# Thirty-one reciprocal roots of the feature norms, computed on GpSimd behind one VectorE step

## The chip, the cores and the metric

The program runs on one core of one Trainium2 chip. The metric is the device time of one execution in microseconds. Five engines work side by side, each through its own queue in order: TensorE (PE; its weight loads are listed as PEld), VectorE (DVE), ScalarE (ACT), GpSimd (POOL) and SyncE (SP), which issues most of the transfers.

## The reference, cut to what matters

Two transformer-like blocks follow each other on 512 tokens of 1024 features in float32, each block two layers deep. The second block also carries a context of 256 tokens. What matters here is the norm over the features that stands in front of and behind nearly every part:

```python
def rms_norm(x, g):
    x32 = x.astype(jnp.float32)
    y = x32 * lax.rsqrt(jnp.mean(x32 * x32, axis=-1, keepdims=True) + EPS)
    return (y * g.astype(jnp.float32)).astype(x.dtype)

for l in range(DEPTH):                       # first block
    h = rms_norm(x, g_norm1[l]) * (1.0 + sc1) + sh1
    ...                                      # two kinds of attention on h
    x = x + gt1 * (merged @ w_out[l])
    h = rms_norm(x, g_norm2[l]) * (1.0 + sc2) + sh2
    ...
    x = x + gt2 * ((jax.nn.silu(a) * v_ff) @ w_down[l])

for i in range(DEPTH):                       # second block
    hx = rmsnorm(x, norm_g[i, 0]) * (1.0 + sc_x) + sh_x
    ...                                      # convolution (i = 0, with a layer norm) or attention (i = 1)
    x = x + g_x * rmsnorm(yx, norm_g[i, 1])
    fx = rmsnorm(x, norm_g[i, 2]) * (1.0 + scf_x) + shf_x
    x = x + gf_x * rmsnorm(swiglu(fx, ffn_w1[i], ffn_w3[i], ffn_w2[i]), norm_g[i, 3])
```

The same is done to the context in the second block, as long as it is needed.

## The kernel before, in words

Activations are kept with the features on the partitions: x is eight tiles of 128 features by 512 tokens. Each matrix product is done three times on rounded halves (high by high, low by high, high by low). So every activation that enters a product is split into hh and hl (`modulate`, lines 268 to 275), and every weight chunk that arrives by DMA is split by `weights`: the high half by ScalarE on L166, the low half by VectorE on L167, up to 128x1024 elements at a time. Products are summed in PSUM by `dense` (L184, L187, L188) and `dense_tok` (L194 to L196).

Most norms are done for 256 tokens at a time, the first half (A) and the second (B) one after the other, or for the context's 256 tokens. A norm has these steps. ScalarE squares each of the eight feature tiles (L226), and VectorE adds the squares of the middle six to the first (L228). `rstd_psum` lets TensorE sum the two remaining tiles over the partitions against a column of 1/1024 (L244), which gives the mean squares as a 128x2 block in PSUM, one column for each 128 tokens. `rsqrt` takes their reciprocal roots with nine VectorE steps (L208 to L217): a scaled copy w, a first guess by arithmetic on the bits as integers, and two steps of iteration, each result written to small tiles rs_w, rs_y, rs_b and rs_c. TensorE then transposes each column, spread over 128 columns, back into a 128x256 block rb in PSUM (L248). `rstd` copies this to SBUF by ScalarE (L255), since GpSimd's share of the products is made from there. `times_rb` multiplies the feature tiles by it: five of eight by VectorE (L266), and the tiles 1, 3 and 5 by ScalarE with the scale (L263) and GpSimd (L264). After a `post_norm` the product is added to x (L828, again tiles 1, 3, 5 on GpSimd) and squared for the norm that comes next; after a `pre_norm` it is shifted, rounded (L274) and its rest taken (L275).

`rstd_psum` is called 31 times: once in front of everything, for 512 tokens at once (four columns, from `emit`), and 30 times for 256. `rsqrt` is called 11 times more, on sums over heads and latents (lines 419, 475, 501, 1156 and 1199), with 8 to 32 columns; those calls stay on VectorE.

The order of the instructions on each engine is not that of the program text. The text gives what depends on what; a planner (`schedule_with_timeline_sim=True`, L1642) lays the instructions out by its own estimates of their times, each on the engine that the text names, and each engine then runs its list in order, waiting on semaphores. So other matmuls may stand between L244 and L248, and other VectorE steps between the nine of a root. Where two tiles have the same tag, `bufs` says how many buffers take turns.

GpSimd's other work is the products L264 and additions L828, sums of gates (L711), parts of the rotary embeddings, and in the convolution the filter tiles (L1009) and the issue of some DMAs (L1014).

Of the kernel before, what the change touches and what calls it, by code (L numbers as in the profile page):

```python
# [12 lines left out]
F32 = mybir.dt.float32  # L13
F32R = mybir.dt.float32r
I32 = mybir.dt.int32
AF = mybir.ActivationFunctionType
ALU = mybir.AluOpType
# [3 lines left out]
P = 128  # L21
# [4 lines left out]
EPS = 1e-6  # L26
# [66 lines left out]
class Core:  # L93
# [105 lines left out]

    def rsqrt(self, v, n, scale=1.0, factor=1.0, step=False):  # L200
        nc = self.nc
        w = self.sm.tile([P, 32], F32, tag="rs_w", name="rs_w", bufs=2)
        y = self.sm.tile([P, 32], F32, tag="rs_y", name="rs_y", bufs=3)
        b = self.sm.tile([P, 32], F32, tag="rs_b", name="rs_b", bufs=2)
        c = self.sm.tile([P, 32], F32, tag="rs_c", name="rs_c", bufs=2)
        w, y, b, c = w[:, :n], y[:, :n], b[:, :n], c[:, :n]
        k = -0.5 / (3.375 * factor) ** 2
        nc.vector.tensor_scalar(w, v, scale * k, EPS * k, op0=ALU.mult, op1=ALU.add)  # L208
        nc.vector.tensor_scalar(y.bitcast(I32), w.bitcast(I32), -0.5, float(0x5F375A86 - 2**22 - 2**30),
                                op0=ALU.mult, op1=ALU.add)  # L210
        nc.vector.tensor_tensor(b, y, y, op=ALU.mult)
        nc.vector.tensor_tensor(b, b, w, op=ALU.mult)
        nc.vector.scalar_tensor_tensor(c, b, 5.0 / 3.0, b, op0=ALU.add, op1=ALU.mult)
        nc.vector.scalar_tensor_tensor(c, c, 1.25, y, op0=ALU.add, op1=ALU.mult)
        nc.vector.tensor_tensor(b, c, c, op=ALU.mult)
        nc.vector.tensor_tensor(b, b, w, op=ALU.mult)
        last = nc.vector.scalar_tensor_tensor(y, b, 2.0 / 3.0, c, op0=ALU.add, op1=ALU.mult)  # L217
        return (y, last) if step else y


    def square_sum(self, pool, sums, x, k):
# [10 lines left out]
    def rstd_psum(self, sums):  # L232

        nc = self.nc
        n = sums[0].shape[-1]
        nt = n // P
        if n <= 256:
            pb = self.at_psum("rb")
            ps = pb[:, 256:]
        else:  # L240
            ps, pb = self.mm_psum("ms"), self.mm_psum("rb")
        for t in range(nt):
            for i, sq in enumerate(sums):
                nc.tensor.matmul(ps[:, t : t + 1], lhsT=sq[:, t * P : (t + 1) * P], rhs=self.mean_col,  # L244
                                 start=(i == 0), stop=(i == len(sums) - 1))
        r, last = self.rsqrt(ps[:, :nt], nt, step=True)
        for t in range(nt):
            nc.tensor.transpose(pb[:, t * P : (t + 1) * P], r[:, t : t + 1].to_broadcast([P, P]), self.ident)  # L248
        return pb[:, :n], last

    def rstd(self, pool, sums):

        pb, _ = self.rstd_psum(sums)
        rb = pool.tile("rb")[:, : pb.shape[-1]]
        self.nc.scalar.copy(rb, pb)  # L255
        return pb, rb
# [1043 lines left out]
def emit(tc, a, out, stop=None):  # L1300
    nc = tc.nc
    with ExitStack() as ctx:
        core = Core(ctx, tc, a)
        dense_psum = ctx.enter_context(ExitStack())
        core.ps = dense_psum.enter_context(core.psum_pool("ps"))
        x, h, c = core.x, core.h, core.const
# [21 lines left out]
        with tc.tile_pool(name="rope", reuse_waits="tile", bufs=1) as rp:  # L1328
# [19 lines left out]
            with tc.tile_pool(name="start", reuse_waits="tile", bufs=1) as pp:  # L1348
                acc = pp.tile([P, S], F32, name="acc")
                for k in range(KD):  # L1350
                    nc.sync.dma_start(out=x[k], in_=a["xT"][k])
                    sq = acc if k == 0 else pp.tile([P, S], F32, tag="sq", name="sq", bufs=3)
                    nc.scalar.activation(sq, x[k], AF.Square)
                    if 0 < k < KD - 1:
                        nc.vector.tensor_tensor(acc, acc, sq, op=ALU.add)
                act = pp.tile([P, KD], F32, name="act")
                nc.scalar.activation(act, core.colrange("c"), AF.Silu)
                wide = pp.tile([P, KD, 32], F32, name="wide")
                nc.vector.tensor_copy(wide, act.unsqueeze(2).to_broadcast([P, KD, 32]))
                each = pp.tile([P, 1], F32, name="each")  # L1360
                nc.vector.tensor_reduce(each, core.ident.rearrange("p (a b) -> p a b", b=32)[:, :, 0], op=ALU.add, axis=AX.X)
                core.idle_products(20)
                rb, _ = core.rstd_psum([acc, sq])
                ups = {t: core.at_psum("lat") for t in range(TOK)}

                def blocks(p):


                    mds = []
                    for which in range(2):  # L1370
                        raw = pp.tile([P, KD, 256], F32, tag="raw", name="rawt", bufs=4)
                        nc.sync.dma_start(out=raw, in_=a["w_ada0"][p, which])
                        md = core.mm_psum("md")
                        for j in range(2):
                            for g in range(4):
                                k = 2 * g + j
                                nc.tensor.matmul(md[32 * g : 32 * g + 32, :256], lhsT=wide[:, k, :], rhs=raw[:, k, :],
                                                 start=(j == 0), stop=(j == 1))
                        rows = pp.tile([P, 256], F32, tag="rows", name="rows0", bufs=2)
                        nc.scalar.copy(rows, md[:, :256])  # L1380
                        mds.append((md, rows))
                    for which, (md, rows) in enumerate(mds):
                        for j in range(2):
                            nc.tensor.matmul(md[:, 256 + j : 257 + j], lhsT=rows[:, j * P : (j + 1) * P], rhs=each,
                                             start=True, stop=True)
                        f = 8 * (1 - which) + 2 * p
                        nc.vector.tensor_tensor(mod[:, f : f + 2], md[:, 256:258], bias0[:, f : f + 2], op=ALU.add)

                for p in range(4):
                    blocks(p)  # L1390
                    ks = slice(2 * p, 2 * p + 2)
                    nc.vector.scalar_tensor_tensor(g1[0][:, ks], mod[:, 8 + 2 * p : 10 + 2 * p], 1.0, core.colrange("g10")[:, ks],
                                                   op0=ALU.add, op1=ALU.mult)
                    wh, wl = core.chunk(a["w_lat"][0, p])
                    for kk in range(2):
                        k = 2 * p + kk
                        xs = pp.tile([P, S], F32, tag="xn", name="xn", bufs=2)
                        nc.vector.scalar_tensor_tensor(xs, x[k], g1[0][:, k : k + 1], rb, op0=ALU.mult, op1=ALU.mult)
                        nc.scalar.activation(h[k][0], xs, AF.Identity, bias=mod[:, k : k + 1])
                        nc.vector.scalar_tensor_tensor(h[k][1], xs, mod[:, k : k + 1], h[k][0], op0=ALU.add, op1=ALU.subtract)  # L1400
                        for t in range(TOK):
                            core.dense_tok(ups[t][:, :448], h[k], slice(t * P, (t + 1) * P),
                                           (wh[:, kk, :], wl[:, kk, :]), k == 0, k == KD - 1)
                crow = core.silu_row(rp, a["c"], "crow")
                core.side = chain(core.modulation_rows(a["w_adat"][0], [crow], bias0, [mod], [48], 16),
                                  core.modulation_rows(a["w_adat"][1], [crow], core.colrange("b_ada1"), [mods[1]], [16]))
                rope_tables(core, pp, cos, sin)
# [229 lines left out]
def build(arrays, stop=None):  # L1637
    nc = bacc.Bacc("TRN2", target_bir_lowering=False, num_devices=1)
    a = {k: nc.dram_tensor(f"in_{k}", v.shape, mybir.dt.from_np(v.dtype), kind="ExternalInput").ap()
         for k, v in arrays.items()}  # L1640
    out = nc.dram_tensor("out_x", (KD, P, S), F32, kind="ExternalOutput").ap()
    with tile.TileContext(nc, schedule_with_timeline_sim=True) as tc:  # L1642
        emit(tc, a, out, stop)
    return nc
# [8 lines left out]
```

## Time and profile before

| | |
|---|---|
| median of three runs | 3121.16 us (3118.2 to 3124.4) |
| the profiled execution | 3128.48 us |
| its span, first to last instruction | 3126.8 us |
| mean granted clock of TensorE in it | 0.977 of full |
| TensorE busy | 3005.0 us |
| VectorE busy | 2153.8 us |
| ScalarE busy | 1386.6 us |
| GpSimd busy | 252.6 us |

The profile is of a single execution. All times within it are microseconds from the span's start. A number in square brackets in a row of the timeline is idle time of that engine just before the instruction, and behind the arrow stands what ended it. TensorE's instructions overlap in the pipeline, so its rows can be longer than their distance. `x2` at the end of a row means that two like instructions are merged in it.

### The profile page before, as it was taken

To read this page: it belongs to the slowest core of one execution; us is meant where nothing else is said; L and a number is where in the kernel's file an instruction comes from. 1 tells how busy PE (TensorE), PEld (TensorE's weight loads), DVE (VectorE), ACT (ScalarE), POOL (GpSimd) and SP (SyncE) were. 2 spreads that over 40 slices of the span, in tenths; PEclk is the share of its full clock that TensorE was granted. 3 is DMA by queue.
4 is the path that set the end of the run, shared out by engine and by line. 5 is a ranking of instruction groups with operands and counts; after the bars stand their busy time and mean duration, and the time that the engine had idled before them with its cause. 6 is when DMAs were issued, how large, how long until landed. Compare 5 with 4: busy or idle time off the path is not lost.

```text
span 3126.8 us, 44991 instructions
## 1 busy us (share of the span) xinstructions
PE 3005.0 (96%) x17004; PEld 2550.3 (82%) x17004; DVE 2153.8 (69%) x4013; ACT 1386.6 (44%) x2532; POOL 252.6 (8%) x336
## 2 busy tenths in 40 slices
PE   8999999999899999999999899999998989999998
PEld 6776888888777698888886699888887767898887
DVE  5774778887676488999789683645578976672336
ACT  3534563335533556343562473222235556653223
POOL 0000200000100020000023120000001510110001
PEclk8999999999999999999999999999999989999999
DMA  6563356454466253333344343433473400243333
GB/s 240 174 218 108 122 169 213 153 180 121 153 208 196 74 173 123 121 107 109 101 150 122 122 151 106 124 98 125 148 238 118 135 28 21 81 149 108 94 101 122
DMA packets 128845, 422.42 MB, mean 135 GB/s; under 512 B 15602, under 2 KB 21362, under 8 KB 127603
## 3 DMA queue, kind: packets, MB, share of 16 engines
q1 hardware_dynamic: 125426, 414.00, 41.1%
q0 software_dynamic: 1280, 2.77, 0.3%
q10 hardware_dynamic: 1920, 2.77, 0.3%
q8 instruction: 134, 2.20, 0.3%
q14 instruction: 85, 0.69, 0.1%
HBM read 411.85 MB, written 2.10 MB: 132 GB/s over the span
## 4 chain that ended last, share of the span: by engine, by line
PE 79%; DVE 11%; ACT 4%; issue 2%; DMA 2%; POOL 1%; ACTq 0%; SPq 0%; DVEq 0%; POOLq 0%
PE dn L184 5%; PE dn L188 5%; PE dn L187 5%; PE up L184 5%; PE up L187 5%; PE up L188 5%; PE pa L184 4%; PE pa L187 4%; PE pa L188 4%; PE pv L188 3%; PE pv L184 3%; PE pv L187 3%; DVE wlo L167 3%; PE g L184 2%; PE g L187 2%
## 5 line engine op out<-in xcount | busy, mean ns | idle before, releaser
L166 ACT CAST whi<-raw 128x1024 fp32r<-128x1024 f32 (+4 forms) x622 | 599.1, 967 | 1017.1 <-PE dn L187 275.2
L167 DVE TENSOR_TENSOR wlo<-raw,whi 128x1024 fp32r<-128x1024 f32 (+4 forms) x622 | 706.3, 1138 | 376.6 <-ACT whi L166 365.0
L184 PE MATMUL dn<-hi,whi 128*128 128x256 f32 (+1 forms) x1088 | 360.5, 334 | 3.9 <-ACT whi L166 1.6
L188 PE MATMUL dn<-hi,wlo 128*128 128x256 f32 (+1 forms) x1088 | 358.4, 332 | 1.2 <-DVE wlo L167 1.0
L187 PE MATMUL dn<-lo,whi 128*128 128x256 f32 (+1 forms) x1088 | 359.2, 331 | 0.2 <-DVE lo L290 0.2
L184 PE MATMUL up<-hh,whi 128*128 128x512 f32 (+1 forms) x800 | 294.3, 369 | 5.9 <-ACT hh L274 3.5
L187 PE MATMUL up<-hl,whi 128*128 128x512 f32 (+1 forms) x800 | 294.0, 368 | 1.1 <-DVE hl L275 1.1
L188 PE MATMUL up<-hh,wlo 128*128 128x512 f32 (+1 forms) x800 | 293.5, 368 | 0.0
L184 PEld LDWEIGHTS dn<-hi,whi 128*128 128x128 f32 x1088 | 205.8, 190 | 26.1 <-ACT whi L166 6.5
L188 PEld LDWEIGHTS dn<-hi,wlo 128*128 128x128 f32 x1088 | 205.9, 190 | 22.6 <-DVE wlo L167 2.0
L187 PEld LDWEIGHTS dn<-lo,whi 128*128 128x128 f32 x1088 | 206.4, 190 | 19.9 <-DVE lo L290 0.4
L313 DVE SCALAR_TENSOR_TENSOR mjunk<-mraw,crow 128x1024 fp32r<-128x1024 f32 (+1 forms) x152 | 185.9, 1223 | 46.8 <-PE g L187 18.9
L264 POOL TENSOR_TENSOR hp<-hp,rb 128x256 f32<-128x256 f32 x90 | 74.5, 840 | 1764.8 <-ACT hp L263 1295.9
L184 PE MATMUL pa<-hh,whi 128*128 128x512 f32 (+1 forms) x496 | 179.4, 362 | 3.4 <-ACT hh L274 3.3
L184 PEld LDWEIGHTS up<-hh,whi 128*128 128x128 f32 x800 | 154.0, 193 | 30.4 <-ACT hh L274 4.1
L187 PE MATMUL pa<-hl,whi 128*128 128x512 f32 (+1 forms) x496 | 178.5, 360 | 0.3
L188 PE MATMUL pa<-hh,wlo 128*128 128x512 f32 (+1 forms) x496 | 177.5, 358 | 0.0
L187 PEld LDWEIGHTS up<-hl,whi 128*128 128x128 f32 x800 | 153.8, 192 | 25.4 <-DVE hl L275 1.8
L188 PEld LDWEIGHTS up<-hh,wlo 128*128 128x128 f32 x800 | 153.7, 193 | 23.9
L188 PE MATMUL pv<-hh,wlo 128*128 128x512 f32 (+1 forms) x432 | 152.0, 352 | 1.1 <-DVE wlo L167 1.1
L184 PE MATMUL pv<-hh,whi 128*128 128x512 f32 (+1 forms) x432 | 151.8, 351 | 0.0
L187 PE MATMUL pv<-hl,whi 128*128 128x512 f32 (+1 forms) x432 | 151.6, 351 | 0.0
(477 smaller groups left out, 6985.3 us busy)
## 6 DMA issues: line engine op xcount, KB each, us to landing
raw<-in_w SPq DMA_DIRECT2D x148, 512.0 KB, 3.5
mraw<-in_w_modt SPq DMA_DIRECT2D x112, 512.0 KB, 4.2
raw<-in_w_up SPq DMA_DIRECT2D x100, 512.0 KB, 3.4
mraw<-in_w_adat SPq DMA_DIRECT2D x80, 512.0 KB, 4.2
raw<-in_w_pw SPq DMA_DIRECT2D x56, 512.0 KB, 3.4
raw<-in_w_down SPq DMA_DIRECT2D x48, 448.0 KB, 3.4
raw<-in_w_g SPq DMA_DIRECT2D x32, 512.0 KB, 4.3
raw<-in_w_out SPq DMA_DIRECT2D x32, 512.0 KB, 3.4
```

The source lines that it names most:

```text
L166: nc.scalar.copy(hi[:, :n], raw[:, :n])
L167: nc.vector.tensor_tensor(lo[:, :n], raw[:, :n], hi[:, :n], op=ALU.subtract)
L184: first = mm(out, lhsT=hi[:, k, :], rhs=xh[:, cols], start=(k == 0), stop=False)
L187: mm(out, lhsT=hi[:, k, :], rhs=xl[:, cols], start=False, stop=False)
L188: self.last = mm(out, lhsT=lo[:, k, :], rhs=xh[:, cols], start=False, stop=(k == n - 1))
L264: nc.gpsimd.tensor_tensor(p, p, rb[1], op=ALU.mult)
L313: behind(nc.vector.scalar_tensor_tensor(junk, raw, 1.0, v, op0=ALU.mult, op1=ALU.mult, accum_out=d[:, f : f + 1]))
```

## The change

`rstd_psum` no longer calls `rsqrt` but a new function, `rsqrt_aside`. It does the scaled copy w on VectorE, since it is read from PSUM, and everything else on GpSimd. The arithmetic is the same, but each of VectorE's three fused steps (add, then multiply) becomes an addition of a constant and a multiplication, so there are eleven GpSimd steps in place of eight on VectorE. Its tiles are four columns wide and have tags of their own, two or three buffers each. The tiles of `rsqrt`, 32 columns wide, get one buffer less each, rs_c apart. Nothing reads the last instruction of the root that `rstd_psum` gave back, and it is gone.

```diff
     def rsqrt(self, v, n, scale=1.0, factor=1.0, step=False):
         nc = self.nc
-        w = self.sm.tile([P, 32], F32, tag="rs_w", name="rs_w", bufs=2)
-        y = self.sm.tile([P, 32], F32, tag="rs_y", name="rs_y", bufs=3)
-        b = self.sm.tile([P, 32], F32, tag="rs_b", name="rs_b", bufs=2)
+        w = self.sm.tile([P, 32], F32, tag="rs_w", name="rs_w", bufs=1)
+        y = self.sm.tile([P, 32], F32, tag="rs_y", name="rs_y", bufs=2)
+        b = self.sm.tile([P, 32], F32, tag="rs_b", name="rs_b", bufs=1)
...
+    def rsqrt_aside(self, v, n):
+        w = self.sm.tile([P, 4], F32, tag="ra_w", name="ra_w", bufs=2)[:, :n]
+        y = self.sm.tile([P, 4], F32, tag="ra_y", name="ra_y", bufs=3)[:, :n]
+        b = self.sm.tile([P, 4], F32, tag="ra_b", name="ra_b", bufs=2)[:, :n]
+        c = self.sm.tile([P, 4], F32, tag="ra_c", name="ra_c", bufs=2)[:, :n]
+        g = self.nc.gpsimd
+        k = -0.5 / 3.375 ** 2
+        self.nc.vector.tensor_scalar(w, v, k, EPS * k, op0=ALU.mult, op1=ALU.add)
+        g.tensor_scalar(y.bitcast(I32), w.bitcast(I32), -0.5, float(0x5F375A86 - 2**22 - 2**30), op0=ALU.mult, op1=ALU.add)
+        g.tensor_tensor(b, y, y, op=ALU.mult)
+        g.tensor_tensor(b, b, w, op=ALU.mult)
+        g.tensor_scalar(c, b, 5.0 / 3.0, None, op0=ALU.add)
+        g.tensor_tensor(c, c, b, op=ALU.mult)
+        g.tensor_scalar(c, c, 1.25, None, op0=ALU.add)
+        g.tensor_tensor(c, c, y, op=ALU.mult)
+        g.tensor_tensor(b, c, c, op=ALU.mult)
+        g.tensor_tensor(b, b, w, op=ALU.mult)
+        g.tensor_scalar(b, b, 2.0 / 3.0, None, op0=ALU.add)
+        g.tensor_tensor(y, b, c, op=ALU.mult)
+        return y
...
-        r, last = self.rsqrt(ps[:, :nt], nt, step=True)
+        r = self.rsqrt_aside(ps[:, :nt], nt)
         for t in range(nt):
             nc.tensor.transpose(pb[:, t * P : (t + 1) * P], r[:, t : t + 1].to_broadcast([P, P]), self.ident)
-        return pb[:, :n], last
+        return pb[:, :n]
```

The two callers of `rstd_psum` (in `rstd` and in `emit`) take one value in place of two.

## Rows read from the trace of the kernel before

**Rows 1.** The page's first part: busy us (share of the span) xinstructions.

```profile
PE 3005.0 (96%) x17004; PEld 2550.3 (82%) x17004; DVE 2153.8 (69%) x4013; ACT 1386.6 (44%) x2532; POOL 252.6 (8%) x336
```

**Rows 2.** Waits of TensorE: who <- for whom: us in total, times, longest us.

```profile
PE rb L244 <- DVE acc L228: 17.9, 5, 5.9
PE rb L248 <- DVE rs_y L217: 7.1, 3, 3.4
```

**Rows 3.** The tile rs_w: durations min/median/max in ns, first and last start.

```profile
L208 DVE TENSOR_SCALAR rs_w<-rb x30: 147/156/160, 387.9 to 3114.5; 128x2 f32<-128x2 f32 x30
```

**Rows 4.** Timelines of two calls: start us, us, engine, line, op, out<-in, shapes.

```profile
391.46 0.15 DVE L217 SCALAR_TENSOR_TENSOR rs_y<-rs_b,rs_c 128x2 f32<-128x2 f32 x1
394.15 0.38 PE L248 MATMUL rb<-ident,rs_y 128*128 128x128 f32 x2
...
3097.16 0.16 DVE L217 SCALAR_TENSOR_TENSOR rs_y<-rs_b,rs_c 128x2 f32<-128x2 f32 x1
...
3099.85 0.38 PE L248 MATMUL rb<-ident,rs_y 128*128 128x128 f32 x2
```

**Rows 5.** Chain of waits that ended last, in pieces: start us, us, what.

```profile
14.93 0.17 DVE rs_w L208
...
1846.48 0.62 DVE rs_c L214
...
3116.03 0.17 DVE rs_y L217
```

**Rows 6.** Timeline of VectorE, the last call's first and last step.

```profile
3114.46 0.16 DVE L208 TENSOR_SCALAR rs_w<-rb 128x2 f32<-128x2 f32 x1 [1.43 <-PE rb L244]
...
3116.03 0.16 DVE L217 SCALAR_TENSOR_TENSOR rs_y<-rs_b,rs_c 128x2 f32<-128x2 f32 x1
```

**Rows 7.** Timeline of GpSimd: steps with two tensors, one behind the other.

```profile
789.04 0.46 POOL L371 TENSOR_TENSOR tabq<-cos,rows 128x128 f32<-128x128 f32 x1 [9.82 <-DMA rows<-in_rows]
789.46 0.46 POOL L371 TENSOR_TENSOR tabq<-sin,rows 128x128 f32<-128x128 f32 x1
...
798.98 1.42 POOL L264 TENSOR_TENSOR hp<-hp,rb 128x256 f32<-128x256 f32 x2 [4.87 <-ACT hp L263]
```

**Rows 8.** Timeline of GpSimd in the first microsecond: fills, then a select.

```profile
0.35 0.10 POOL L1638 MEMSET const-float32-1.0<- 128x1 f32 x1
...
0.81 0.20 POOL masks.py:197 MEMSET ident<- 128x128 f32 x1 [0.29 <-POOLq L1638]
1.09 0.29 POOL masks.py:199 TENSOR_SCALAR_AFFINE_SELECT ident<-ident 128x128 f32<-128x128 f32 x1
```

**Rows 9.** Timelines of GpSimd and VectorE where each is slowed.

```profile
427.79 2.71 POOL L264 TENSOR_TENSOR hp<-hp,rb 128x256 f32<-128x256 f32 x2 [26.62 <-ACT hp L263]
427.81 1.22 DVE L167 TENSOR_TENSOR wlo<-raw,whi 128x1024 fp32r<-128x1024 f32 x1
...
2498.03 1.30 POOL L1185 TENSOR_TENSOR stk<-qf,stk 128x512 f32<-128x512 f32 x1
2498.13 1.22 DVE L212 TENSOR_TENSOR rs_b<-rs_b,rs_w 128x8 f32<-128x8 f32 x1
```

**Rows 10.** Timeline of TensorE: transposes that waited for a root.

```profile
16.73 1.11 PE L248 MATMUL rb<-ident,rs_y 128*128 128x128 f32 x4 [1.84 <-DVE rs_y L217]
...
797.40 0.69 PE L248 MATMUL rb<-ident,rs_y 128*128 128x128 f32 x2 [3.42 <-DVE rs_y L217]
```

**Rows 11.** Timeline of VectorE behind the call at 1597.3.

```profile
1598.99 1.23 DVE L167 TENSOR_TENSOR wlo<-raw,whi 128x1024 fp32r<-128x1024 f32 x1
...
1600.47 1.22 DVE L167 TENSOR_TENSOR wlo<-raw,whi 128x1024 fp32r<-128x1024 f32 x1
```

**Rows 12.** Three stretches: busy us (x) of each engine, granted clock, DMA.

```profile
1840.00:1850.00 10.00, 5.85 (x25) 5.16 (x25) 8.74 (x32) 5.74 (x16) 2.33 (x3) 0.59 0.29 102
2412.00:2419.00 7.00, 4.12 (x16) 3.37 (x16) 5.47 (x24) 3.51 (x9) 1.42 (x2) 0.50 0.06 24
2737.00:2747.00 10.00, 8.13 (x38) 7.44 (x38) 8.72 (x33) 6.27 (x15) 3.44 (x5) 0.54 0.19 54
```

More of the change, by code (lines that the diff above doesn't have):

```diff
@@ L245, in rstd_psum @@
                                  start=(i == 0), stop=(i == len(sums) - 1))
-        r, last = self.rsqrt(ps[:, :nt], nt, step=True)
+        r = self.rsqrt_aside(ps[:, :nt], nt)
         for t in range(nt):
             nc.tensor.transpose(pb[:, t * P : (t + 1) * P], r[:, t : t + 1].to_broadcast([P, P]), self.ident)
-        return pb[:, :n], last
+        return pb[:, :n]
     def rstd(self, pool, sums):
-        pb, _ = self.rstd_psum(sums)
+        pb = self.rstd_psum(sums)
         rb = pool.tile("rb")[:, : pb.shape[-1]]
@@ L1362, in emit @@
                 core.idle_products(20)
-                rb, _ = core.rstd_psum([acc, sq])
+                rb = core.rstd_psum([acc, sq])
                 ups = {t: core.at_psum("lat") for t in range(TOK)}
```

## The prediction

> **What bounds the kernel now.** I read the page first: TensorE is busy 96% of the span, VectorE 69%, GpSimd 8% [rows 1]. So a step costs time only where TensorE waits for it. TensorE's waits come next [rows 2]: for a finished reciprocal root (L248) it waited 7.1 us in three places, for the sums in front of one (L244) 17.9 us in five. The change touches 31 calls, 30 of two columns [rows 3] and the first one of four. In the timelines I set the end of L217 against the start of the transposes L248 in each call. In 21 of the 31 the transposes came 1.2 us or more behind the root, with other matmuls between; the first is at 391.6 to 394.15, the last at 3097.3 to 3099.85 [rows 4]. In the other ten the root is nearly or wholly waited for. Along the chain of waits I added up the pieces named after the roots' tiles: 52 pieces, from 14.93 to 3116.03, make 8.2 us for these 31 calls [rows 5], of which 1.6 us lie in the first call, 1.6 us in the last, 1.0 us near 795, and nearly all the rest where two norms follow each other. That, not VectorE's total, is what can be won.
>
> **What goes from VectorE.** The last call runs alone: nine steps, 3114.46 to 3116.19, one every 0.196 us, 0.16 us each [rows 6]. Eight of nine go: 31 x 8 x 0.196 = 48.6 us of VectorE's 2153.8. TensorE has other work during most of that, so it counts as nothing except below.
>
> **What comes to GpSimd.** Eleven steps, as each fused VectorE pair becomes two: seven with two tensors, four with one. No row shows such a step at two columns; the nearest bound it. Two tensors at 128 columns take 0.46 us, one every 0.42; at 256 columns two take 1.42 us together, one every 0.70 [rows 7]. So a column costs (0.70 - 0.42)/128 = 2.2 ns, and two columns about 0.46 - 126 x 0.0022 = 0.18 us. With one tensor, a select of 128 columns takes 0.29 us and a fill of one column 0.10 us [rows 8]: I take 0.14. Each step reads what the one before it wrote. The one such pair at hand, fill then select of the same tile, starts 0.08 us after the first one's end (0.81 + 0.20 to 1.09) [rows 8]; I add that to all. The root alone is then 0.16 (VectorE's step) + 0.1 (crossing over, estimated from that 0.08) + 7 x 0.26 + 4 x 0.22 - 0.08 = 2.9 us, against 1.73 now: 1.1 us later. Bounds: at 0.10 us for each step, as that fill, and nothing between them, it would be 0.16 + 0.1 + 1.1 = 1.4 us, 0.4 us earlier; at 0.46 + 0.08 for each, 6.1 us, 4.4 us later. I stay near 2.9: the steps have two columns, but they depend on each other.
>
> The Trainium skill (GPSIMD Engine Reference, section on performance versus the Vector engine) gives a measured ratio of 1.96 between GpSimd and VectorE for a two-tensor add. By that an estimate is 0.16 x 1.96 = 0.31 us for each step, a root of 4.5 us, and the uncovered calls below would cost 2.8 us each in place of 1.1.
>
> **What stretches it.** Two of GpSimd's products L264 take 1.42 us together [rows 7], but 2.71 from 427.79, when VectorE ran a 1.22 us weight split (L167) beside them [rows 9]. The other way round, VectorE's step L212 of 0.16 us took 1.22 while GpSimd held a 1.30 us step [rows 9]. So a step of the chain that meets a VectorE step with two tensors from SBUF waits out what is left of it. I laid the 2.9 us chain over VectorE's own steps behind each of the 31 starts: it comes to about 3.9 us in the mean (2.9 to 5.9), where the present chains, with what is queued between their steps, take 3.7.
>
> This is the rule of the Trainium skill (SBUF — State Buffer, who interferes with whom): one shared pair of ports, held for the whole instruction. The trace agrees, by the two rows just named.
>
> **The sum.**
> First call (four columns): TensorE idles 1.84 us for it [rows 10] with nothing else ready: +1.1.
> Last call: TensorE, ScalarE's copy and the whole tail stand behind it, VectorE is otherwise idle [rows 6]: +1.1.
> Call at 793.7: idle 3.42 us now [rows 10], but that chain holds a weight split and four bias additions between its steps; on GpSimd it takes 3.8 in place of 3.6: +0.2.
> Call at 1597.3: the transposes follow the root by 1.0 us and two weight splits come right behind it, the first at 1598.99 [rows 11]. Laid over them the chain is up to 5.3 us long and 2.6 late; the order will be planned anew, so I take +1.0.
> Three places where a pre-norm and the next half's post-norm follow each other (1840, 2412, 2737): by the same overlay the first root is some 0.8 us later at its transposes, beyond the 0.5 us of slack that these have. But the second runs on VectorE between the first half's products (L266, L275), and in two of the three VectorE, not TensorE, is on the chain: the second root's pieces are 1.83 us of it at 1844 to 1849 (one of its nine pieces in rows 5), and 1.40 at 2739. Without the step that stays they are 1.66 and 1.23, and half of that should reach the end, since TensorE has the first half's matmuls to do meanwhile: 3 x 0.8 - 1.4 = +1.0.
> The 21 covered calls: 0. Their cover is TensorE's other matmuls; each would cost about 1.1 us without it.
> Together +4.4 us. The profiled execution is 3128.48 us (span 3126.8); with the change 3132.9. The median shown is 3121.16, 7.3 us lower; the same difference there gives 3125.6; I round to 3125.
> The smaller buffer counts of the VectorE version cost nothing: one engine runs those steps in order anyway.
>
> **Rivals.** *The cover goes* (slower). Instructions are placed by a planner. If it prices GpSimd's steps without their waits on VectorE's, it puts the transposes about where the 2.9 us chain ends, and TensorE stands still for the 1.1 us by which the real one is longer, in the 21 covered calls: 23 us and the 4.4, so 3148.6. Behind each L248 stands ScalarE's copy L255, and behind that weight casts. Against it: the slack is 2.4 us in many calls now, and ScalarE waits little for L264, so its prices are not tight. It decides where slack falls under 1 us.
> *GpSimd's queue* (slower). In the paired places, and near 1184, the second chain stands on GpSimd in front of the L264 products of the first half, which TensorE needs one by one; 2.9 us less some 1 us until the next tile is needed, four times: 7.6 + 4.4, so 3133. It happens if the planner ranks the root first.
> *VectorE's relief tells* (faster). The 8.2 us on the chain lose 8/9 = 7.3, the ends give 2.2 back, and the idle stretches shorten. The granted clock's mean is 0.59, 0.50 and 0.54 of full over 10, 7 and 10 us there [rows 12], between its levels of 1.2 and 2.4 GHz: 4.1 + 3.5 + 4.6 = 12.2 us lost, and half of it back makes 11 in all: 3110. Against it: VectorE may pay in waits on GpSimd's steps [rows 9] what it saves.
>
> **How the numbers follow.** What a measurement can tell from no change here is 0.2%, 6.2 us: 3114.9 to 3127.4. My forecast, 46%: about 3125, own range 3117 to 3132; it holds 2% of faster, 39% of same, 5% of slower. Cover goes, 17%, all slower. Queue, 14%: 12 slower, 2 same. Relief, 23%: 18 faster, 5 same. So faster 0.20, same 0.46, slower 0.34. The range runs from the relief, 3108, to just short of the full loss of cover, 3145.
>
> **What would show it.** GpSimd busy up by some 55 us (31 x 11 x 0.16) and more by waits, VectorE down by about 40 (248 x 0.16), L248's waits at the first and last call longer by 1 us each, the steps 0.2 to 0.3 us apart where VectorE rests and one to each VectorE step where it does not. Wrong would be: roots under 1.7 us or over 4.5 in the last call; TensorE's waits for L248 over 20 us in all (cover gone); the clock's low stretches gone (relief).

## The result, and the profile after

The changed kernel takes 3135.8 us (median of five runs, 3131.07 to 3140.48) against 3121.16 for the kernel before (five runs, 3118.2 to 3124.57): a ratio of 1.0052, interval 1.0041 to 1.0062. That is 14.6 us slower, above the 0.2% that the prediction set as the limit of "no change". 3135.8 lies inside the predicted range (3108 to 3145) and outside the likeliest case's own (3117 to 3132). The profiled execution is the median one: 3135.8 us, span 3134.1.

Lines move with the 23 new ones: L208 to L217 are still VectorE's root for the other eleven calls; the feature norms' root is now L229 (VectorE) and L230 to L240 (GpSimd). The sums L244 are L267, the transposes L248 are L271, the products L264 are L287.

The page's first part, kernel after (busy us, share of the span, instructions):

```profile
PE 2999.3 (96%) x17004; PEld 2539.5 (81%) x17004; DVE 2115.0 (67%) x3765; ACT 1385.4 (44%) x2532; POOL 348.5 (11%) x677
```

Against [rows 1], VectorE lost 38.8 us and GpSimd gained 95.9 in 341 instructions. TensorE was idle for 134.8 us of its span, 121.8 before; its busy time fell by 5.7 us, but the execution of before that was profiled had run at a granted clock of 0.977 in the mean and this one at 0.981, and over the runs on record 0.001 of this clock goes with about 2.2 us within one kernel (an estimate: one straight line through all runs, with a level for each kernel). That is some 9 us, so the two profiles differ by less than the two medians.

Waits of TensorE, kernel after (who <- for whom: us in total, times, longest us):

```profile
PE rb L271 <- POOL ra_y L240: 20.5, 9, 4.3
PE rb L267 <- DVE acc L251: 11.3, 3, 7.0
```

Against [rows 2], the wait for roots has grown from 7.1 to 20.5 us, the wait for the sums that VectorE adds up in front of a root has shrunk from 17.9 to 11.3. Over all rows of this view, TensorE's waits add up to 110.3 us before and 123.5 after.

The last call, GpSimd's timeline (start us, us, engine, line, op, out<-in, shapes), then TensorE's:

```profile
3120.49 0.19 POOL L230 TENSOR_SCALAR ra_y<-ra_w 128x2 int32<-128x2 int32 x1 [8.06 <-DVE ra_w L229]
3120.77 0.19 POOL L231 TENSOR_TENSOR ra_b<-ra_y 128x2 f32<-128x2 f32 x1
...
3121.32 0.21 POOL L233 TENSOR_SCALAR ra_c<-ra_b 128x2 f32<-128x2 f32 x1
...
3123.32 0.19 POOL L240 TENSOR_TENSOR ra_y<-ra_b,ra_c 128x2 f32<-128x2 f32 x1
```

```profile
3123.57 0.69 PE L271 MATMUL rb<-ident,ra_y 128*128 128x128 f32 x2 [3.37 <-POOL ra_y L240]
```

With VectorE's step at 3120.24 the root takes 3.27 us, in place of 1.73 [rows 6]. A step takes 0.19 us with two tensors and 0.21 with one (the integer step L230 0.19), and the next starts 0.08 us after its end. Over all calls (durations in ns, min/median/max, first and last start):

```profile
L233 POOL TENSOR_SCALAR ra_c<-ra_b x31: 215/216/1230, 16.9 to 3121.3; 128x2 f32<-128x2 f32 x30, 128x4 f32<-128x4 f32 x1
...
L238 POOL TENSOR_TENSOR ra_b<-ra_b,ra_w x31: 194/197/1207, 19.2 to 3122.7; 128x2 f32<-128x2 f32 x30, 128x4 f32<-128x4 f32 x1
```

The medians are the undisturbed steps; each line has some of over a microsecond, 35 of the 341 steps took more than half of one.

The first call shows what stretches it. GpSimd's timeline of its eighth step and the one behind, then VectorE's, then TensorE's:

```profile
18.07 1.02 POOL L237 TENSOR_TENSOR ra_b<-ra_c 128x4 f32<-128x4 f32 x1
19.17 0.20 POOL L238 TENSOR_TENSOR ra_b<-ra_b,ra_w 128x4 f32<-128x4 f32 x1
```

```profile
17.95 1.09 DVE L167 TENSOR_TENSOR wlo<-raw,whi 128x896 fp32r<-128x896 f32 x1 [2.00 <-ACT whi L166]
```

```profile
20.01 0.90 PE L271 MATMUL rb<-ident,ra_y 128*128 128x128 f32 x3 [4.26 <-POOL ra_y L240]
```

A step of 0.20 us takes 1.02 since a weight split of VectorE began just before it. TensorE waits 4.26 us, where it waited 1.84 [rows 10].

The 19th call had cover in the kernel before. TensorE's last sum and the transposes there, kernel before; then the same in the kernel after:

```profile
1864.25 0.36 PE L244 MATMUL rb<-mean_col,sqx 128*128 128x1 f32 x2
1869.34 0.38 PE L248 MATMUL rb<-ident,rs_y 128*128 128x128 f32 x2
```

```profile
1868.01 0.36 PE L267 MATMUL rb<-mean_col,sqx 128*128 128x1 f32 x2
1873.33 0.43 PE L271 MATMUL rb<-ident,ra_y 128*128 128x128 f32 x2 [2.71 <-POOL ra_y L240]
```

The distance is 5 us in both, but before it was filled with other matmuls; after, the order has put those ahead of the sums. Twelve us from 1864 before and from 1868 after (busy us (x) of each engine, granted clock, DMA):

```profile
1864.00:1876.00 12.00, 11.95 (x100) 11.75 (x100) 10.42 (x24) 7.92 (x15) 1.68 (x2) 1.00 0.64 191
```

```profile
1868.00:1880.00 12.00, 7.60 (x47) 6.87 (x47) 8.91 (x18) 6.50 (x15) 5.31 (x14) 0.86 0.34 120
```

TensorE is idle for 4.4 us in place of 0.05, and its granted clock is 0.86 in the mean of these 12 us, in place of 1.00. Setting the same matmuls of the two traces against each other, 7 us are lost from 1815 to 1885.

The surprise lies where there are no roots. A stretch of the feed-forward part, TensorE alone, before, then after:

```profile
510.00:540.00 30.00, 30.00 (x134) 1.00 0.71 228
```

```profile
510.00:540.00 30.00, 30.00 (x129) 1.00 0.73 240
```

TensorE is busy throughout, at the full granted clock, and does five matmuls fewer in the same time: the 512-column ones follow each other every 234 ns in place of 227. I added up, over all 512-column matmuls that have the next one 228.5 to 246 ns behind them, what lies above 227: 6.2 us before (6.0 in another profile of it), 17.3 after. I call this the excess. Of its growth by 11.1 us, 8.9 are in the products dn, which stream the tiles hi and lo of the feed-forward pools, and 1.3 in the products br, which stream tiles hi and lo as well; the products up, which stream hh and hl, hold 0.1 to 0.2 us in both.

### The profile page after: what moved, and what is told of

The parts are those of the page before. It is cut to its first block, busy times and chain, and to the rows that moved or that the text cites. A ratio compares the mean times of both kernels' runs of the same rounds, so it can differ in the third digit from the quotient of the medians.

```text
span 3134.1 us, 45068 instructions
## 1 busy us (share of the span) xinstructions
PE 2999.3 (96%) x17004; PEld 2539.5 (81%) x17004; DVE 2115.0 (67%) x3765; ACT 1385.4 (44%) x2532; POOL 348.5 (11%) x677
## 4 chain that ended last, share of the span: by engine, by line
PE 79%; DVE 9%; ACT 4%; DMA 3%; issue 2%; POOL 2%; ACTq 0%; SPq 0%; DVEq 0%; POOLq 0%
PE dn L188 5%; PE dn L184 5%; PE dn L187 5%; PE up L188 5%; PE up L184 5%; PE up L187 5%; PE pa L184 4%; PE pa L187 4%; PE pa L188 4%; PE pv L184 3%; PE pv L188 3%; PE pv L187 3%; DVE wlo L167 3%; PE g L184 2%; PE g L187 2%
## 5 line engine op out<-in xcount | busy, mean ns | idle before, releaser
L230 POOL TENSOR_SCALAR ra_y<-ra_w 128x2 int32<-128x2 int32 (+1 forms) x31 | 9.7, 312 | 1551.6 <-DVE ra_w L229 1551.4
```

Of the source, the lines that this page charges most:

```text
L230: g.tensor_scalar(y.bitcast(I32), w.bitcast(I32), -0.5, float(0x5F375A86 - 2**22 - 2**30), op0=ALU.mult, op1=ALU.add)
```

## The experiments

Theory A is that the time follows from late roots; B, that the planner's new order loses it; C, that GpSimd's steps disturb the other engines; D, added after the first four runs, that it is the place of the tiles in SBUF. E, added for the last runs, is that the planner, given longer roots, spends their cover elsewhere. Each job had the kernel before beside it: 3123.0 (11 runs), 3121.2 (28) and 3119.8 (21) in the three jobs; ratios are to that.

**The kernel before again.**

> The kernel before once more, for a second profile of it: the profiled execution of before took 3128.48 us, 7.3 us more than the median of its timed runs, so where the 14.6 us lie cannot be read from it alone. Theory A (root latency: the root takes 3.3 to 5 us on GpSimd in place of 1.7 to 3.7, and TensorE waits for it in the calls without cover): TensorE's wait for L248 is again 7 us in three places, and the second profile is faster than the first in stretches that hold no norm. Rival B (the planner's new order costs it): the same. If the profile shows TensorE waiting 15 us or more for L248 in the kernel before, A has no ground.

3120.77 us. TensorE's waits for roots (7.0 us in three places) and the excess (6.0) are as in the first profile of it; the waits for VectorE's sums are 16.3 us, 17.9 in the first.

**The second iteration left out on GpSimd** (seven GpSimd steps in place of eleven; the result is less exact, and that work is left out):

```diff
-        c = self.sm.tile([P, 4], F32, tag="ra_c", name="ra_c", bufs=2)[:, :n]
+        c = self.sm.tile([P, 4], F32, tag="ra_c", name="ra_c", bufs=3)[:, :n]
...
-        k = -0.5 / 3.375 ** 2
+        k = -0.5 / 1.5 ** 2
...
-        g.tensor_tensor(b, c, c, op=ALU.mult)
-        g.tensor_tensor(b, b, w, op=ALU.mult)
-        g.tensor_scalar(b, b, 2.0 / 3.0, None, op0=ALU.add)
-        g.tensor_tensor(y, b, c, op=ALU.mult)
-        return y
+        return c
```

> The second step of iteration is left out (the scale constant is adapted, so the root is good to 1e-4 only): seven GpSimd steps in place of eleven, 4 x 0.29 = 1.15 us less for each root. Theory A: TensorE's waits for the root, 20.5 us in nine places, fall by about 1.1 us in each, to 10 or 12 us, and the time falls by 8 to 10 us, to 3126 to 3128. Rival B (the new order of the planner, not the length): no such slope; the time lands anywhere within 6 us of 3136. Rival C (collisions between GpSimd's and VectorE's steps): a third of the steps goes, so a third of the 14.6: 3131.

3112.16 us, ratio 0.9962 (0.9947 to 0.9976): faster than both kernels. TensorE's waits for the root, however, did not shrink:

```profile
PE rb L267 <- POOL ra_c L236: 23.6, 8, 5.3
PE rb L263 <- DVE acc L247: 7.4, 2, 7.0
```

The profiled run was the longest of its six (3120.45). The time follows the root's length, but not by this row alone: waits for VectorE's sums went down as well (7.4 us, 11.3 in the changed kernel), and TensorE's waits add up to 108.3 us, 2 below the kernel before.

**Four GpSimd steps more** in each root:

```diff
+        for _ in range(4):
+            g.tensor_scalar(b, b, 0.0, None, op0=ALU.add)
```

> Four more dependent GpSimd steps (adding zero) ahead of the last: 4 x 0.30 = 1.2 us more for each root, the result as before. Theory A: at least nine uncovered calls grow by 1.2 us each, 11 us, and some of those with 1.3 to 1.5 us of slack lose a little: 3146 to 3150, TensorE's waits for the root 31 us or more. Rival B: within 6 us of 3136, with no sign. Rival C: 4/11 of 14.6 more, 3141.

3148.39 us, ratio 1.0085 (1.0072 to 1.0098), 0.0033 or 10 us above the changed kernel's ratio.

```profile
PE rb L273 <- POOL ra_y L242: 27.5, 8, 5.6
```

So a longer root costs, as A has it: four steps of some 0.29 us are 1.2 us a call, and 10 us are that much in nine of 31 calls. TensorE's idle time grew by 11.8 us, from 134.8 to 146.6 in the profiles. The four runs had a lower clock (0.9765 in the mean, 0.9816 in the five of the changed kernel), so the 10 us may not be the steps' price alone.

**VectorE's root used, GpSimd's run beside it** with its result unused:

```diff
-        r = self.rsqrt_aside(ps[:, :nt], nt)
+        r = self.rsqrt(ps[:, :nt], nt)
+        self.rsqrt_aside(ps[:, :nt], nt)
```

> The root of the kernel before on VectorE, and beside it the whole of the changed one (one VectorE step and eleven GpSimd steps), whose result nothing reads. All of GpSimd's steps and their collisions with VectorE's are there, the latency is not. Theory A: 3121 to 3125 (31 VectorE steps more, most of them covered). Rival C: 3131 to 3137, as slow as the changed kernel or nearly. Rival B: anywhere, since this is planned anew too.

3134.77 us, ratio 1.0042 (1.0028 to 1.0055): most of the loss with no root late, so A alone can't account for it.

```profile
PE rb L272 <- DVE rs_y L217: 7.3, 3, 3.7
```

The wait for roots is that of the kernel before, but the excess is 17.3 us, as after the change. That made me compare where the compiled programs place their tiles. The nine 32-column tiles of VectorE's root (128 bytes a partition each) are now six, and the nine new 4-column tiles take 32 bytes each: 1152 bytes became 1056. All tiles of the pools stacked behind the small one, among them hi and lo of the feed-forward pools, stand 96 bytes lower (64 lower with the short root, whose ra_c has one buffer more); x, hh, hl and the weights' tiles don't move.

**The changed kernel at the old addresses:**

```diff
-        y = self.sm.tile([P, 4], F32, tag="ra_y", name="ra_y", bufs=3)[:, :n]
+        y = self.sm.tile([P, 16], F32, tag="ra_y", name="ra_y", bufs=3)[:, :n]
```

> The changed kernel with ra_y's tile 16 columns wide instead of 4 (only the first n are used). The three buffers then take 64 bytes a partition each instead of 32, and every tile that is placed behind the small-tile pool stands at the address that it had in the kernel before; the change alone had moved all of those 96 bytes down. No instruction differs from the changed kernel's. Theory D (the shift by 96 bytes slows the 512-column matmuls in the feed-forward stages, summed excess over 227 ns 17.3 us in the changed kernel, 6.0 before): the excess falls to about 6 us and the time by about 11, to 3123 to 3127, what is left being the later roots at ten calls. Theories A (root latency alone) and C (GpSimd's steps disturb the others): addresses do nothing, 3133 to 3138 and an excess of 17.

3129.76 us, ratio 1.0027 (1.0015 to 1.0038). The excess is 6.4 us, as D has it; in the same stretch, TensorE:

```profile
510.00:540.00 30.00, 30.00 (x134) 1.00 0.78 249
```

The order of the instructions on every engine is that of the changed kernel, so that only the addresses differ. The time fell by less than the 11 us of excess: 0.0025 of ratio, 8 us (3 to 13 with both intervals). What is left, 8.6 us (5 to 12 by the interval), belongs to GpSimd's roots: that they come late, the order planned for them, or their steps beside the other engines'.

```profile
PE rb L271 <- POOL ra_y L240: 19.0, 9, 3.9
PE rb L267 <- DVE acc L251: 11.4, 3, 7.0
```

**The kernel before, 96 bytes lower,** with the same instructions:

```diff
-        b = self.sm.tile([P, 32], F32, tag="rs_b", name="rs_b", bufs=2)
+        b = self.sm.tile([P, 32], F32, tag="rs_b", name="rs_b", bufs=1)
...
-    v = sm.tile([P, 8], F32, tag="v_lat", name="v_lat", bufs=1)
+    v = sm.tile([P, 16], F32, tag="v_lat", name="v_lat", bufs=1)[:, :8]
```

> The kernel before, with rs_b in one buffer instead of two and v_lat's tile 16 columns wide (8 used): all tiles behind the small-tile pool stand 96 bytes lower, as in the changed kernel; the roots stay on VectorE, and no instruction is added or taken out. Theory D: the excess of the 512-column matmuls rises from 6 to about 17 us and the time by about 11, to 3131 to 3136. Theories A and C: nothing here has changed for them, 3119 to 3125 with an excess of 6.

3130.69 us, ratio 1.0035 (1.0022 to 1.0047): 9.5 us lost with VectorE's roots where they were. With one buffer of rs_b less the planner has put 124 of TensorE's 17004 matmuls, and some steps of the other engines, in other places, all between 2437 and 2770 us; the rest of the order is that of the kernel before. Excess 17.2 us; of it dn 10.6 (1.7 before), up as before. TensorE in the same stretch:

```profile
510.00:540.00 30.00, 30.00 (x129) 1.00 0.74 241
```

The stretch shown lies outside the reordered part, so D's mechanism is shown: the place of the tiles alone slows these matmuls. Over the profiles, the excess is 6.0 to 6.4 us in the seven at the old addresses and 17.2 to 17.4 in the four that are 96 bytes lower. What it costs at the end is less clear. The five runs here had a granted clock of 0.9778 in the mean, the kernel before in the same job 0.9808, and at 2.2 us for each 0.001 some 6 of the 9.5 us go with the clock. The first profile of the kernel before, at 0.977 as this one, took 3128.48 us, 2.2 less. Whether the shift or chance lowered the clock is open.

**GpSimd's unused root at the old addresses** (the same edit of ra_y):

> VectorE's root is used; GpSimd's whole root runs beside it with its result unused, as in the run that took 3134.8 us; the one edit against that run is ra_y's tile 16 columns wide, which puts all tiles behind the small-tile pool back at the addresses of the kernel before. Theory D: time falls by about 11 to 3121 to 3126, excess about 6 us. Theory C (the 341 added GpSimd instructions and 31 VectorE ones cost the 12 us by standing beside the others): stays at 3131 to 3138.

3125.49 us, ratio 1.0019 (1.0006 to 1.0031), excess 6.2. The order is that of the run before at the shifted addresses, and the shift made 0.0023 of the 0.0042. The rest, 2 to 10 us, fits a cost of GpSimd's steps beside the others (C), but I have not located it, and these runs had a lower clock too (0.9792 in the mean, 0.9808 in the kernel before):

```profile
PE rb L272 <- DVE rs_y L217: 7.0, 3, 3.3
```

**The short root at the old addresses:**

```diff
-        w = self.sm.tile([P, 4], F32, tag="ra_w", name="ra_w", bufs=2)[:, :n]
+        w = self.sm.tile([P, 16], F32, tag="ra_w", name="ra_w", bufs=2)[:, :n]
```

> GpSimd's root with the second iteration left out (seven GpSimd steps instead of eleven), as in the run that took 3112.2 us with all tiles behind the small-tile pool 64 bytes lower than before; here ra_w's tile is 16 columns wide, and they stand at the addresses of the kernel before. Theory D: the excess falls from 15.0 to about 6 us and the time by about 9, to 3101 to 3106. Theories A and C: no change, 3108 to 3116.

3114.91 us, ratio 0.9984 (0.9974 to 0.9995). The excess fell from 15.0 to 6.3, the time did not: its ratio is above that of the shifted short root. D's forecast failed here. The runs of the shifted one had a higher granted clock (0.9823 in the mean, against 0.9806), worth some 4 us at 2.2 us for each 0.001; whether the clock's rise came from the shift or by chance is open. Set to the same clock in this way (an estimate), the shift costs 8.6 us in the changed kernel, 4.1 beside the unused root, 3.9 in the kernel before and 0.2 in the short root, each with a standard error of 1.1 to 1.3. The shifted one of the pair had the higher clock in two of the four and the lower in two, which speaks for chance but doesn't show it. Against the full root at the same addresses and in the same job, the four steps are worth 15 us, which is 1.2 us in twelve or thirteen calls.

**GpSimd's root only in the ten calls that the prediction called uncovered,** and, as a second kernel, only in the 21 others; both at the old addresses:

```diff
+TEN = (0, 4, 6, 10, 16, 17, 22, 26, 27, 30)
...
-        r = self.rsqrt_aside(ps[:, :nt], nt)
+        call, self.roots = self.roots, self.roots + 1
+        root = self.rsqrt_aside if call in TEN else self.rsqrt
+        r = root(ps[:, :nt], nt)
```

> At the addresses of the kernel before (ra_y's tile 16 columns wide), the root runs on GpSimd only in the ten calls that the prediction called uncovered (the 1st, 5th, 7th, 11th, 17th, 18th, 23rd, 27th, 28th and 31st in the program's order), on VectorE in the other 21. With GpSimd in all 31 at these addresses it was 8.6 us over the kernel before (3129.8 against 3121.2), and TensorE's transposes waited 21.0 us for roots in place of 7.0. Theory A (the ten carry the cost: 1.1 us or more later each at the places where TensorE stands): 3126 to 3130, waits of the transposes 14 us or more. Theory E (the planner, given longer roots, spends the cover elsewhere, as in the 19th call, which had 2.4 us of slack before and is waited for 2.7 us now): the ten make 3122 to 3126. Theory C (each GpSimd chain costs by standing beside the others): 10/31 of 8.6, 3123 to 3125.

> At the addresses of the kernel before, the complement: the root runs on GpSimd in the 21 calls that the prediction called covered, on VectorE in the ten others. Theory A (covered calls cost nothing, and VectorE is relieved where its queue makes roots of 10 to 12 us, as in the 8th and 13th call): 3117 to 3122, no wait of the transposes for GpSimd over 0.5 us. Theory E: the 19th call's wait stays at 2 to 3 us and TensorE stands still there for some 4 us in all, 3124 to 3128. Theory C: 21/31 of 8.6, 3126 to 3128.

The ten: 3119.93 us, ratio 1.0003 (0.999 to 1.0016). The 21: 3118.94, ratio 0.9996 (0.9982 to 1.001). Waits of TensorE in the ten, then in the 21:

```profile
PE rb L271 <- DVE acc L255: 18.2, 6, 5.9
PE rb L277 <- POOL ra_y L244: 15.6, 7, 4.3
```

```profile
PE rb L271 <- DVE acc L255: 14.2, 4, 7.0
PE rb L277 <- DVE rs_y L221: 8.0, 4, 3.7
...
PE rb L277 <- POOL ra_y L244: 1.0, 1, 1.0
```

The waits fall out as A says: nearly all of them belong to the ten, and the 21 wait 1.0 us for GpSimd. The times don't: neither part is measurably slower, and together they miss the 8.6 us. For the ten the interval reaches from -3 to +5 us, which holds the predicted +4.4 but not A's 3126 to 3130; its profiled run (3129.1) was the longest of eleven. In the 21 the 19th call no longer stops TensorE. Setting the same matmuls against the kernel before as above, from its 1815 to its 1885, all 31 at the old addresses lose 7 us there, the ten 4 and the 21 0.6. So more than half of this loss comes with the ten, of which the 17th and 18th call stand right in front, and the rest only with all 31: the parts don't simply add up. In this one place the order spends the cover as E has it, though E's forecast that the 19th call would stop TensorE in the 21 failed. By the medians, of the forecasts in time only A's for the 21 held; for the ten the interval also reaches into E's and C's. Why the ten's time doesn't show its 4 us, and whether jobs differ by that much, was not tried further.

**Other shifts of the kernel before,** one run each: 128 bytes lower (rs_b in one buffer) and 32 higher (that and v_lat 48 columns wide).

> The kernel before with rs_b in one buffer instead of two: all tiles behind the small-tile pool stand 128 bytes lower, and nothing else changes. A shift of 96 bytes took the summed excess of the 512-column matmuls over 227 ns from 6.0 to 17.2 us, one of 64 bytes to 15.0. Theory D1 (what counts is the offset of the streamed tile against the weights' tile modulo 128 bytes, which this shift keeps): excess 6 us. Theory D2 (any shift against the unshifted tiles does it, or modulo 256 and more counts): excess 12 to 18 us.

> The kernel before with rs_b in one buffer and v_lat's tile 48 columns wide (8 used): all tiles behind the small-tile pool stand 32 bytes higher, their offset modulo 128 is 64 as with the shift of 96 bytes down, and nothing else changes. Theory D1 (offset modulo 128 bytes): excess 17 us, as with the 96 bytes. Theory D3 (how far the tiles are from their old place, 32 bytes against 64 and 96): excess between 6 and 15.

Excess 14.3 and 14.6 us. TensorE in the same stretch, 128 lower, then 32 higher:

```profile
510.00:540.00 30.00, 30.00 (x130) 1.00 0.69 225
```

```profile
510.00:540.00 30.00, 30.00 (x130) 1.00 0.75 243
```

All four shifts tried (-128, -96, -64, +32) do it, so an offset modulo 128 bytes (D1) is not what counts, and neither is the distance alone (D3): 32 bytes make as much excess as 128. The old place is better than every other one tried. What is special about it is open: in the old place hi starts at byte 131744 and the first weight tile at 82336, a multiple of 256 apart, but a shift of 256 was not run. The single times, 3139.5 and 3123.6, differ by 16 us at equal excess, with clocks of 0.975 and 0.980; they show how little one run's time says.

## Why the prediction was right and wrong

**The step that failed** is the last sentence of the sum: "The smaller buffer counts of the VectorE version cost nothing". It looked at who waits for a buffer, and there it was right. But tile counts and sizes also set the addresses of everything placed behind them, and 96 bytes made TensorE's 512-column matmuls slower by 11 us in all, in stretches that have no root. At the end, putting the tiles back takes 0.0025 of ratio, 8 us, from the changed kernel itself: about half of the 14.6. The price is not the same everywhere: 7 us in the pair with the unused root and 9.5 in the kernel before (some 4 each at an equal clock); the short root was 7 us faster with the shift, and level at an equal clock. Why less than 11 arrives is only argued: in the profiles, the time lost in feed-forward parts is partly made up right behind them, where TensorE otherwise waits for weights.

**The roots' sum**, +4.4, was of the right sign and too small: 8.6 us at the old addresses (5 to 12). Term by term, from the profile after:

- Step size. 0.18 and 0.14 us were predicted with 0.08 between; 0.19, 0.21 and 0.08 came. Only the one-tensor step was off, and 4 x 0.07 us make most of the difference between 2.9 and 3.27. The Trainium skill's ratio of 1.96 for GpSimd against VectorE (GPSIMD Engine Reference, performance versus the Vector engine) gave 0.31 us a step and a root of 4.5; here, at two columns, it is 0.19 to 0.16, and the trace decides.
- Stretch by VectorE: a chain of 3.9 us predicted in the mean of 31 calls, 4.7 measured (3.27 to 7.7; 3.7 before). GpSimd's busy time shows it: 31 x (7 x 0.194 + 4 x 0.213) is 68 us; its 341 steps took 101.5, and the difference is steps held up. The rule on shared ports that the prediction took from the Trainium skill (SBUF — State Buffer, who interferes with whom) agrees with the step of 1.02 us at 18.07.
- First call: +1.1 predicted, +2.4 measured (4.26 against 1.84). The root has grown into a weight split that used to come behind it. The overlay was made for all calls, but this term was priced without it. In the profile at the old addresses the wait is 3.46 us, +1.6: where the split falls is not the same in every execution.
- Last call: +1.1 predicted, +1.5 measured. The call at 793.7: +0.2 and +0.7. The one at 1597: +1.0 and +1.5.
- The three pairs: +1.0 predicted. Their waits for roots grew by 2.2 us.
- The 21 covered calls: 0 predicted. 18 of them wait for nothing new; the 8th (1.6 us), the 19th (2.7 us, and 7 us lost around it) and the 25th (0.7 us) do. So the rival in which the cover goes came true in three places of 21; in the 19th call by an order that spends the covering matmuls ahead of the sums. That the planner would do this was not among the rival's reasons, which had it price GpSimd's steps too low. Its sign, over 20 us of waits in all, was met by half a microsecond.
- VectorE's relief, the rival on the fast side, may be there too: 6.6 us less waiting for VectorE's sums (5.0 against the second profile of before), though the new order can have done this as well. It pays half of the 13.4 us of new waits for roots, and 13.4 - 6.6 = 6.8 is near the 8.6 us left at the old addresses. The clock's low stretches stayed.

**The chances.** The range held the time by the width left for the loss of cover, not for the cause that added most, so that 3135.8 fell inside it is in good part luck. At the old addresses 8.6 us would still have been above the limit of 6.2, though its interval reaches below.

No full root tried beats the kernel before: the best, GpSimd in the 21 covered calls, is within its interval of it. Both short roots beat both kernels by leaving out the second iteration; whether VectorE's root cut in the same way would do better was not run.

## What to carry to other kernels

When a change alters the size or number of small tiles, compare the addresses of all other tiles before and after; if they moved, pad until they don't, and only then time the change. A loss in stretches that the change doesn't touch, with the engine busy and its clock unchanged, points there. A chain of small dependent steps moved to another engine must be laid over the steps of the engine that can hold it up in every call, and cover counted in one order of the program is not cover in the next. Before a few microseconds are put down to a cause, compare the granted clocks of the runs: here they differed between kernels by as much as the effect.

## What the runs showed of the hardware

- A 512-column matmul of the split float32 products in a dense row starts every 227 ns, or every 234 when the streamed tile stands 96 bytes lower than its old place (233 at 64 lower, 232 at 128 lower, 234 at 32 higher), at a granted clock of 1.00 each time; TensorE did 129 in place of 134 in 30 us.
- A GpSimd step on two columns takes 0.19 us with two tensors and 0.19 to 0.21 with one, hardly more than VectorE's 0.16, with 0.08 us between dependent steps. One that meets a VectorE weight split of 1.1 to 1.2 us waits it out and takes up to 1.23 us.
- The mean granted clock of whole runs, one kernel on one chip, went from 0.978 to 0.984, and the kernel before from 3129.3 to 3112.2 us with it: about 2.2 us for each 0.001 within one kernel, over all runs on record. A difference under 10 us between a few runs can be the clock's.
